# Another order of the first loads in a two-layer trunk: one modulation piece ahead of x, small tables moved to SyncE's queue

## The chip, the cores and the metric

The kernel runs on 1 core of one Trainium2 chip. The metric is the device time of one execution in microseconds (us): the median of several runs. One more execution is taken with the hardware profiler; the trace and every row below come from that one. The engines are TensorE (PE in the rows, with its weight loads as PEld), VectorE (DVE), ScalarE (ACT), GpSimd (POOL) and SyncE (SP, which only issues transfers here).

## The reference, cut to what matters

What is computed is a trunk of two layers over 128 context tokens and 512 latent tokens (640 columns), model width 1024. The part that the change touches is the beginning of layer 0:

```python
def rms_norm(x, g):
    xf = x.astype(jnp.float32)
    y = xf * lax.rsqrt(jnp.mean(xf * xf, axis=-1, keepdims=True) + EPS)
    return (y * g.astype(jnp.float32)).astype(x.dtype)

def modulation(cvec, w, b):
    m = jax.nn.silu(cvec) @ w + b
    return jnp.split(m[:, None, :], N_MOD, axis=-1)
...
        hp = rms_norm(xp, norm1) * (1 + sc1_p) + sh1_p
        hs = rms_norm(xs, norm1) * (1 + sc1_s) + sh1_s
        if layer % 2 == 0:
            mp, new_k, new_v = attn_mixer_context(hp, l0_w_in, ...)
            ms = attn_mixer_latent(hs, cache_l0_k, cache_l0_v, l0_w_in, ...)
```

`attn_project` multiplies the normalised x with `l0_w_in` and splits the columns into q, k, v of grouped-query attention (mixer A, with a rotary on the latent tokens' q and k) and q, k, v of a neighbourhood attention (mixer B). Then come the output projection, a squared-ReLU MLP, and layer 1 (a gated delta rule and another MLP).

## The kernel before

**Two phases.** `net_kernel` (L1551) builds two phases. The first (L1559 to L1564) holds the setup, the first norm and modulation, and all of layer 0's attention (`attn_layer`, L586). It is built with `schedule_with_timeline_sim=True`: a scheduler sets, when the kernel is built, the order of instructions on each engine from its own estimate of times, so the order isn't the order of the code. The second phase is in the order of the code. Between them is a barrier: TensorE's first matmul of phase two waits for the branch at L78 that ends phase one.

**The first norm.** `first_norm` (L310) works feature-major: x arrives as 8 tiles of 128 x 640 (320 KB each; tile k holds features 128k to 128k+127, columns 0 to 511 are latent and 512 to 639 context). Its loads go to SyncE's queue, one behind the other: x (L320), then the modulation weights for shift and scale in 4 pieces of 2 MB (L324; "m0" to "m3" below, in a pool of 3 buffers, so m3 waits until m0 is read). Between m1 and m2 the call `use(None, None)` puts the first 256 columns of `w_in0`, the k and v columns of mixer A (`proj_w`, L608 to L612; 1 MB, "w0" below, then w1, w2, ... for the q columns). Each w is split into a high part (ACT, L228) and a low part (DVE, L229), in two halves, t_79/t_80 and t_81/t_82 for w0.

**The arithmetic of the head.** The squares of x are summed (`sumsq`, ACT L295 and L298, DVE L299, into `acc`), a matmul with ones sums over partitions (L306, bank kq), and ACT makes the reciprocal root `rs` (L307, L308). A piece s of the modulation (64 small matmuls, L340, bank md; a copy, L343; a transposition, L345; gains on DVE, L348 and L350) gives shift and scale for features k = 2s and 2s+1. For k below 4, DVE multiplies x by gain and rs (L357), ACT adds the shift and rounds to the high part (L358), DVE makes the low part (L359). For k from 4 on DVE multiplies by rs first (L363), gain and shift follow (L366 on DVE, L369 on ACT), and `split_act` (L235, L236) makes the two parts. The parts of k are t_59+2k (high) and t_60+2k (low).

**The projection.** Every k goes straight into the k/v projection: for each of 5 token blocks three matmuls (L618 high by high, L619 high x by low w, L620 low x by high w), into three banks that stay open over all k: pj_122 (blocks 0 and 1), pj_123 (2 and 3), pj_124 (4). Beside them the first q columns are projected block by block, into pj_699 (block 0), md_738 (block 1), md_777 (block 2), and pj_816 (block 3). The banks named pj are four buffers in rotation, so pj_816 is written where pj_122 was: it waits until `ev_kv` has read blocks 0 and 1 out (split of v on ACT L605, the norm of k: ACT L681, L684, L685, DVE L683, L686; then rotary, L705 and L708, and a transposition on PE, L735).

**Tables and cache.** The rotary table `rope` (256 KB, L662), and the context's k (`cka`, L713, 128 KB) and v (`cv`, L715, 64 KB) are loaded by ACT's queue at the kernel's start. DVE multiplies `rope` with the k and q gains into two tables (L668, L673); the tables are first needed by the rotary behind the k norm.

**Further on** in phase one: mixer A, then mixer B from about 262 us, in whose course further modulation weights (`t<-in_mod_w_dram`, matmuls of L170) are loaded and used. Scores are L981 to L985, their transpositions L789, outputs L842, L924, L1007 and L1017.

Of the kernel before, what the change touches and what calls it, by code (L numbers as in the profile page):

```python
# [11 lines left out]
F32 = mybir.dt.float32  # L12
# [6 lines left out]
P = 128  # L19
D = 1024  # L20
NK = D // P
TS = 512
TP = 128
T = TS + TP
# [25 lines left out]
class Net:  # L50
# [259 lines left out]
    def first_norm(self, use):  # L310

        nc = self.nc
        w = self.i["mod_w0"]
        with ExitStack() as c:
            mp = c.enter_context(self.tc.tile_pool(name="m0", bufs=3))
            self.open_norm(c)
            xt, ws = [], []
            for k in range(NK):
                t = self.xp.tile([P, T], F32, tag="x", name="x")
                nc.sync.dma_start(out=t, in_=self.i["xT"][k * P:(k + 1) * P, :])  # L320
                xt.append(t)
            for s in range(4):
                wt = mp.tile([P, NK, 512], F32, tag="w", name="w")
                nc.sync.dma_start(out=wt, in_=w[:, s * 512:(s + 1) * 512].rearrange("(k p) c -> p k c", p=P))  # L324
                ws.append(wt)
                if s == 1:
                    use(None, None)
            for k in range(NK):
                self.sumsq(k, xt[k], 0, T)
            rs = self.np.tile([P, T], F32, tag="rs", name="rs", bufs=1)  # L330
            for hf in range(2):
                self.rsqrt(rs, hf, "kq")
            g = self.gain[0, 0]
            by_block = lambda z: z.rearrange("p (i k) -> p k i", i=2)
            for s in range(4):
                two = slice(2 * s, 2 * s + 2)
                ps = self.bank("md")
                for k in range(NK):
                    for q in range(4):
                        nc.tensor.matmul(ps[32 * q:32 * q + 32, 0:P], lhsT=self.cs[:, k, :], rhs=ws[s][:, k, q * P:(q + 1) * P],  # L340
                                         start=(k == 0), stop=(k == NK - 1))
                m = self.sm.tile([P, P], F32, tag="modm", name="modm", bufs=1)
                nc.scalar.copy(m, ps[:, 0:P])  # L343
                pt = self.bank("md")
                nc.tensor.transpose(out=pt[:, 0:P], in_=m, identity=self.ident)  # L345
                ptv = pt[:, 0:P].rearrange("p (k i x) -> p k i x", k=2, i=2)
                for v in range(2):
                    nc.vector.tensor_tensor(out=by_block(self.modT[0][:, 0:16, v])[:, two], in0=ptv[:, :, :, v],  # L348
                                            in1=by_block(self.vec("modb0")[:, 0:16])[:, two], op=ALU.add)
                    nc.vector.scalar_tensor_tensor(out=g[:, two, v], in0=self.modT[0][:, 8 + 2 * s:10 + 2 * s, v], scalar=1.0,  # L350
                                                   in1=self.vec("n1_0")[:, two], op0=ALU.add, op1=ALU.mult)
                for k in (2 * s, 2 * s + 1):
                    if k < 4:
                        x, (hi, lo) = xt[k], self.act[2 * k:2 * k + 2]
                        for v, o in ((0, slice(0, TS)), (1, slice(TS, T))):
                            sh = self.mod_vec(0, 0, k, v)
                            nc.vector.scalar_tensor_tensor(out=x[:, o], in0=x[:, o], scalar=g[:, k, v:v + 1], in1=rs[:, o], op0=ALU.mult, op1=ALU.mult)  # L357
                            nc.scalar.activation(hi[:, o], x[:, o], AF.Identity, bias=sh)  # L358
                            nc.vector.scalar_tensor_tensor(out=lo[:, o], in0=x[:, o], scalar=sh, in1=hi[:, o].bitcast(F32),  # L359
                                                           op0=ALU.add, op1=ALU.subtract)  # L360
                        use(k, (hi, lo))
                        continue
                    nc.vector.tensor_tensor(out=xt[k], in0=xt[k], in1=rs, op=ALU.mult)  # L363
                    for v, o in ((0, slice(0, TS)), (1, slice(TS, T))):
                        if k % 2:
                            nc.vector.tensor_scalar(out=xt[k][:, o], in0=xt[k][:, o], scalar1=g[:, k, v:v + 1],  # L366
                                                    scalar2=self.mod_vec(0, 0, k, v), op0=ALU.mult, op1=ALU.add)
                        else:
                            nc.scalar.activation(xt[k][:, o], xt[k][:, o], AF.Identity, scale=g[:, k, v:v + 1], bias=self.mod_vec(0, 0, k, v))  # L369
                    use(k, self.split_act(k, xt[k]))  # L370
# [215 lines left out]
def attn_layer(n):  # L586
# [44 lines left out]
    with ExitStack() as outer:  # L631
# [27 lines left out]
        with c:  # L659
            tp = c.enter_context(tc.tile_pool(name="qt", bufs=2))  # L660
            rope = tp.tile([P, 4, 128], F32, name="rope", bufs=1)
            nc.scalar.dma_start(out=rope, in_=I["rope"])  # L662

            tabs = {}
            for nm in ("gqa_r", "gkan_r"):
# [44 lines left out]

            nc.scalar.dma_start(out=vall[:, 5, :], in_=I["ctxv"][:, 128:640])
            ck = tp.tile([P, KVA, 128], F32, name="cka", bufs=1)
            nc.scalar.dma_start(out=ck, in_=I["ctxk"][:, 0:KVA])  # L713
            cv = tp.tile([P, 128], F32, name="cv", bufs=1)
            nc.scalar.dma_start(out=cv, in_=I["ctxv"][:, 0:128])  # L715
            split_v(va[5], cv)
            kd = [tp.tile([P, KVA, 2, HD], F32, name=f"ka{blk}", bufs=1) for blk in range(NB)]

# [1026 lines left out]
```

## Time and profile before

| what | value |
|---|---|
| median of 3 runs | 1807.68 us |
| lowest and highest run | 1805.96 and 1809.21 us |
| the profiled execution's own time | 1806.72 us |
| its span, first to last instruction | 1805.0 us |
| mean granted TensorE clock over the span | 0.992 of full speed |
| TensorE busy | 1726.7 us, 96 % of the span |
| DVE, ACT, GpSimd busy | 70 %, 51 %, 12 % |
| bytes moved | 187.22 MB, mean 104 GB/s |
| first matmul of phase two | at 344.57 us |

How to read it: TensorE is busy nearly all the time, so the end is set by where TensorE idles or runs at the lower of its two clocks (1.2 instead of 2.4 GHz, shown as 0.50 and 1.00 of full speed). In the page's rows a slice is 45 us long; only the first, with a busy share of five tenths, is far from full, and the DMA engines are full there and nearly idle afterwards. The change lies in that slice.

### The profile page before, as it was taken

The page shows a single profiled execution, that of the slowest core. Times are in us where ns is not written, and L with a number is a line of the kernel's source. Part 1 is how long each engine was busy: PE and PEld are TensorE (multiplying, and loading weights), DVE is VectorE, ACT ScalarE, POOL GpSimd, SP SyncE. Part 2 cuts the span into 40 slices and gives each one's busy share as a digit, 9 for nine tenths or more (in the row PEclk, how much of TensorE's full clock was granted, in tenths as well). Part 3 has the DMA queues.
Part 4 walks back from the last instruction along what each step waited for, and adds up shares of the span by engine and source line. Part 5 has one row for each costly group of instructions (what it writes and reads, how often), then busy time and mean ns, then how long its engine had stood idle before and what let it go on. Part 6 is the DMA issues. An engine that isn't in the chain of part 4 may idle for free. (4 is left out here: it accounts for less than half of the span.)

```text
span 1805.0 us, 34898 instructions
## 1 busy us (share of the span) xinstructions
PE 1726.7 (96%) x14120; PEld 1621.2 (90%) x14120; DVE 1266.6 (70%) x2554; ACT 921.0 (51%) x2037; POOL 215.1 (12%) x218
## 2 busy tenths in 40 slices
PE   5999998899999999999989999999999999999999
PEld 4898886699999999999888878878999999999999
DVE  6766557469988678787697877776449957465562
ACT  4555565345345171554756656656636427164360
POOL 0233314100000000000232222222110000000000
PEclk9999998999999999999999999999999999999999
DMA  9101059314433435254122222232232423222231
GB/s 351 57 27 50 26 157 284 132 52 164 164 117 125 135 101 200 73 178 162 48 48 70 50 48 69 51 82 73 66 129 94 140 63 101 72 71 94 68 104 52
DMA packets 174994, 187.22 MB, mean 104 GB/s; under 512 B 48457, under 2 KB 152137, under 8 KB 174833
## 3 DMA queue, kind: packets, MB, share of 16 engines
q1 hardware_dynamic: 170272, 175.05, 30.9%
q0 software_dynamic: 1408, 5.41, 0.9%
q10 hardware_dynamic: 3152, 4.52, 0.8%
q8 instruction: 111, 1.82, 0.4%
q14 instruction: 51, 0.41, 0.1%
HBM read 170.97 MB, written 11.37 MB: 101 GB/s over the span
## 5 line engine op out<-in xcount | busy, mean ns | idle before, releaser
L228 ACT CAST t<-t 128x1024 fp32r<-128x1024 f32 x169 | 176.5, 1048 | 243.0 <-PE p L246 135.7
L229 DVE TENSOR_TENSOR t<-t 128x1024 fp32r<-128x1024 f32 x169 | 207.3, 1230 | 56.8 <-ACT t L228 55.9
L245 PE MATMUL dn<-t 128*128 128x320 f32 x648 | 207.7, 320 | 3.7 <-PEq L78 3.1
L246 PE MATMUL dn<-t 128*128 128x320 f32 x648 | 208.2, 321 | 0.0
L247 PE MATMUL dn<-t 128*128 128x320 f32 x648 | 207.4, 320 | 0.0
L246 PE MATMUL p<-hl,t 128*128 128x320 f32 x448 | 138.5, 309 | 0.0
L245 PEld LDWEIGHTS dn<-t 128*128 128x128 f32 x648 | 122.5, 189 | 7.9 <-issue 5.8
L246 PE MATMUL dn<-hl,t 128*128 128x320 f32 x416 | 129.0, 310 | 0.0
L192 DVE SCALAR_TENSOR_TENSOR ma<-t,ma 128x1024 f32<-128x1024 f32 x98 | 122.8, 1279 | 6.0 <-DMA t<-in_mod_w_dram 5.8
L246 PEld LDWEIGHTS dn<-t 128*128 128x128 f32 x648 | 122.6, 189 | 4.0 <-issue 2.5
L247 PEld LDWEIGHTS dn<-t 128*128 128x128 f32 x648 | 122.6, 189 | 3.4 <-issue 2.5
L413 DVE SCALAR_TENSOR_TENSOR x<-p,t,x 128x192 f32<-128x192 f32 (+2 forms) x154 | 53.1, 385 | 101.0 <-PE p L247 101.0
L245 PE MATMUL p<-hh,t 128*128 128x320 f32 x392 | 121.3, 310 | 0.0
L247 PE MATMUL p<-hh,t 128*128 128x320 f32 x392 | 121.2, 309 | 0.0
L245 PE MATMUL dn<-hh,t 128*128 128x320 f32 x376 | 116.8, 311 | 0.0
L247 PE MATMUL dn<-hh,t 128*128 128x320 f32 x376 | 116.2, 309 | 0.0
L228 ACT CAST wxh<-t 128x1024 fp32r<-128x1024 f32 x49 | 51.3, 1047 | 85.9 <-PE p L246 40.6
L413 DVE SCALAR_TENSOR_TENSOR x<-dn,t,x 128x320 f32<-128x320 f32 (+1 forms) x86 | 44.9, 525 | 62.4 <-PE dn L247 51.8
L246 PEld LDWEIGHTS p<-hl,t 128*128 128x128 f32 x448 | 84.1, 188 | 0.0
L246 PEld LDWEIGHTS dn<-hl,t 128*128 128x128 f32 x416 | 78.1, 188 | 1.0 <-issue 0.8
L783 POOL TENSOR_TENSOR p<-p,smx 128x640 f32<-128x640 f32 (+1 forms) x48 | 63.8, 1338 | 114.9 <-DVE smx L782 99.3
L245 PEld LDWEIGHTS p<-hh,t 128*128 128x128 f32 x392 | 73.6, 188 | 0.8 <-issue 0.4
(599 smaller groups left out, 5195.7 us busy)
## 6 DMA issues: line engine op xcount, KB each, us to landing
t<-in_mlp_w_dram SPq DMA_DIRECT2D x64, 1024.0 KB
t<-in_mod_w_dram SPq DMA_DIRECT2D x40, 1024.0 KB, 6.4
t<-in_w_qkv_dram SPq DMA_DIRECT2D x12, 1024.0 KB
t<-in_w_in_dram SPq DMA_DIRECT2D x9, 1024.0 KB, 5.4
w<-in_mod_w_dram SPq DMA_DIRECT2D x4, 2048.0 KB, 16.3
t<-in_w_out_dram SPq DMA_DIRECT2D x8, 1024.0 KB, 5.7
bias<-in_biasx_dram SPq DMA_DIRECT2D x8, 512.0 KB, 6.7
t<-in_w_z_dram SPq DMA_DIRECT2D x4, 1024.0 KB
```

Of the source, the lines that this page charges most:

```text
L192: nc.vector.scalar_tensor_tensor(out=acc[v], in0=wt[:, k], scalar=c, in1=acc[v], op0=ALU.mult, op1=ALU.add)
L228: nc.scalar.copy(hi, raw)
L229: nc.vector.tensor_tensor(out=lo, in0=raw, in1=hi.bitcast(F32), op=ALU.subtract)
L245: self.nc.tensor.matmul(ps, lhsT=hi[:, k, :], rhs=xh[:, ts_], start=(k == 0), stop=False)
L246: self.nc.tensor.matmul(ps, lhsT=hi[:, k, :], rhs=xl[:, ts_], start=False, stop=False)
L247: self.nc.tensor.matmul(ps, lhsT=lo[:, k, :], rhs=xh[:, ts_], start=False, stop=(k == NK - 1))
L413: nc.vector.scalar_tensor_tensor(out=xout[:, a:b], in0=ps[:, a - o:b - o], scalar=self.mod_vec(layer, idx, k, v), in1=xin[:, a:b], op0=ALU ...
L783: nc.gpsimd.tensor_tensor(out=pv, in0=pv, in1=sm.unsqueeze(2).broadcast_to([P, nb, w]), op=ALU.mult)
```

## The change

`first_norm` writes its loads in another order, and three small loads go from ACT's queue to SyncE's. The piece of modulation m0 is loaded first, then x, then w0, then m1, m2, m3. The code of one piece of modulation is put into a function (same instructions), and m0's is called ahead of the sums of squares. The transfers' sizes and the arithmetic are the same. Since phase one's order is chosen when the kernel is built, every engine's order in phase one changes.

```diff
             xt, ws = [], []
-            for k in range(NK):
-                t = self.xp.tile([P, T], F32, tag="x", name="x")
-                nc.sync.dma_start(out=t, in_=self.i["xT"][k * P:(k + 1) * P, :])
-                xt.append(t)
-            for s in range(4):
+            g = self.gain[0, 0]
+            by_block = lambda z: z.rearrange("p (i k) -> p k i", i=2)
+
+            def load(s):
                 wt = mp.tile([P, NK, 512], F32, tag="w", name="w")
                 nc.sync.dma_start(out=wt, in_=w[:, s * 512:(s + 1) * 512].rearrange("(k p) c -> p k c", p=P))
                 ws.append(wt)
-                if s == 1:
-                    use(None, None)
-            for k in range(NK):
-                self.sumsq(k, xt[k], 0, T)
-            rs = self.np.tile([P, T], F32, tag="rs", name="rs", bufs=1)
-            for hf in range(2):
-                self.rsqrt(rs, hf, "kq")
-            g = self.gain[0, 0]
-            by_block = lambda z: z.rearrange("p (i k) -> p k i", i=2)
-            for s in range(4):
+
+            def modulation(s):
+
                 two = slice(2 * s, 2 * s + 2)
                 ps = self.bank("md")
...
+
+            load(0)
+            for k in range(NK):
+                t = self.xp.tile([P, T], F32, tag="x", name="x")
+                nc.sync.dma_start(out=t, in_=self.i["xT"][k * P:(k + 1) * P, :])
+                xt.append(t)
+            use(None, None)
+            for s in range(1, 4):
+                load(s)
+            modulation(0)
+            for k in range(NK):
+                self.sumsq(k, xt[k], 0, T)
+            rs = self.np.tile([P, T], F32, tag="rs", name="rs", bufs=1)
+            for hf in range(2):
+                self.rsqrt(rs, hf, "kq")
+            for s in range(4):
+                if s:
+                    modulation(s)
                 for k in (2 * s, 2 * s + 1):
...
-            nc.scalar.dma_start(out=rope, in_=I["rope"])
+            nc.sync.dma_start(out=rope, in_=I["rope"])
...
-            nc.scalar.dma_start(out=ck, in_=I["ctxk"][:, 0:KVA])
+            nc.sync.dma_start(out=ck, in_=I["ctxk"][:, 0:KVA])
             cv = tp.tile([P, 128], F32, name="cv", bufs=1)
-            nc.scalar.dma_start(out=cv, in_=I["ctxv"][:, 0:128])
+            nc.sync.dma_start(out=cv, in_=I["ctxv"][:, 0:128])
```

In the changed kernel line numbers are shifted: L320 is L348, L324 is L323, L340 to L350 are L332 to L342, L357 to L369 are L367 to L379, and everything from `attn_layer` on is 10 lines later.

**SyncE's queue**, from its first transfer on (x, w of modulation, t of `w_in0` = w0, w1, ...). Before:

```order
L101 DMA craw<-in_cT_dram 128x16
L102 DMA t<-in_vecs_dram 128x333
L320 DMA x<-in_xT_dram 128x640 x8
L324 DMA w<-in_mod_w_dram 128x8x512 x2
L611 DMA t<-in_w_in_dram 128x8x256
L324 DMA w<-in_mod_w_dram 128x8x512
L611 DMA t<-in_w_in_dram 128x8x256
L324 DMA w<-in_mod_w_dram 128x8x512
L611 DMA t<-in_w_in_dram 128x8x256 x3
```

And now:

```order
L101 DMA craw<-in_cT_dram 128x16
L102 DMA t<-in_vecs_dram 128x333
L323 DMA w<-in_mod_w_dram 128x8x512
L348 DMA x<-in_xT_dram 128x640 x8
L621 DMA t<-in_w_in_dram 128x8x256
L323 DMA w<-in_mod_w_dram 128x8x512 x2
L672 DMA rope<-in_rope_dram 128x512
L723 DMA cka<-in_ctxk_dram 128x256
L725 DMA cv<-in_ctxv_dram 128x128
L621 DMA t<-in_w_in_dram 128x8x256
L323 DMA w<-in_mod_w_dram 128x8x512
L621 DMA t<-in_w_in_dram 128x8x256 x3
```

m0 has moved ahead of x, w0 ahead of m1, and rope, cka and cv stand behind m2 and ahead of w1; m3 has the same bytes ahead of it as before.

**DVE in the head**: the rotary tables (`tbgqa_r`, `tbgkan_r`) against the sums of squares (`acc`) and the normalised x. Before, from the setup's last instruction on:

```order
L107 TENSOR_TENSOR t<-craw,ce 128x8x2
L668 TENSOR_TENSOR tbgqa_r<-rope,t 128x4x64
L673 TENSOR_TENSOR tbgqa_r<-rope,t 128x4x16 x4
L668 TENSOR_TENSOR tbgkan_r<-rope,t 128x4x64
L673 TENSOR_TENSOR tbgkan_r<-rope,t 128x4x16 x4
L299 TENSOR_TENSOR acc<-acc,sq 128x640 x7
L363 TENSOR_TENSOR x<-x,rs 128x640 x4
L348 TENSOR_TENSOR t<-md,t 128x2x2 x2
```

And now, from the first normalised k on (`acc` and w0's low parts stand ahead of this):

```order
L373 TENSOR_TENSOR x<-x,rs 128x640 x4
L369 SCALAR_TENSOR_TENSOR t<-x,t 128x512
L369 SCALAR_TENSOR_TENSOR t<-x,t 128x128
L369 SCALAR_TENSOR_TENSOR t<-x,t 128x512
L369 SCALAR_TENSOR_TENSOR t<-x,t 128x128
L678 TENSOR_TENSOR tbgqa_r<-rope,t 128x4x64
L683 TENSOR_TENSOR tbgqa_r<-rope,t 128x4x16 x4
L678 TENSOR_TENSOR tbgkan_r<-rope,t 128x4x64
L683 TENSOR_TENSOR tbgkan_r<-rope,t 128x4x16 x4
L340 TENSOR_TENSOR t<-md,t 128x2x2 x2
L342 SCALAR_TENSOR_TENSOR t<-t 128x2 x2
```

The rotary tables moved from the very start to a place between the low parts of k = 0, 1 and the gains (L340) of k = 2, 3.

**PE at the k/v projection's last features**, k = 6 (t_71, t_72) and k = 7 (t_73, t_74). Before, where k = 6 begins:

```order
L620 MATMUL md_738<-t_79,t_70 128x256
L618 MATMUL md_777<-t_83,t_59 128x256
L619 MATMUL md_777<-t_84,t_59 128x256
L620 MATMUL md_777<-t_83,t_60 128x256
L618 MATMUL md_777<-t_83,t_61 128x256
L618 MATMUL pj_122<-t_81,t_71 128x256
L619 MATMUL pj_122<-t_82,t_71 128x256
```

And now:

```order
L629 MATMUL md_777<-t_84,t_65 128x256
L630 MATMUL md_777<-t_83,t_66 128x256
L628 MATMUL md_777<-t_79,t_67 128x256
L629 MATMUL md_777<-t_80,t_67 128x256
L630 MATMUL md_777<-t_79,t_68 128x256
L628 MATMUL md_777<-t_79,t_69 128x256
L629 MATMUL md_777<-t_80,t_69 128x256
L630 MATMUL md_777<-t_79,t_70 128x256
L628 MATMUL pj_122<-t_81,t_71 128x256
L629 MATMUL pj_122<-t_82,t_71 128x256
```

Fourteen more of the matmuls of q's block 2 (md_777) now stand ahead of k = 6 of the k/v projection. From the last matmul into pj_122 to the first transposition of k (L735, now L745), behind which pj_816 begins, there were 38 matmuls; now there are 21.

## Rows read from the trace of the kernel before

**Rows 1.** The page: busy us, share of the span, instructions, of TensorE.

```profile
PE 1726.7 (96%) x14120; PEld 1621.2 (90%) x14120; DVE 1266.6 (70%) x2554; ACT 921.0 (51%) x2037; POOL 215.1 (12%) x218
```

**Rows 2.** TensorE in time: start, us, instruction, idle before it and who ended it.

```profile
14.66 2.50 PE L306 MATMUL kq<-acc,t 128*128 128x320 f32 x4 [14.66 <-DVE acc L299]
17.83 3.20 PE L340 MATMUL md<-w,t 128*32 128x128 f32 x64 [0.67 <-DMA w<-in_mod_w_dram]
...
23.36 3.22 PE L340 MATMUL md<-w,t 128*32 128x128 f32 x64 [1.54 <-DMA w<-in_mod_w_dram]
27.34 0.62 PE L618 MATMUL pj<-t 128*128 128x256 f32 x3 [0.75 <-ACT t L228]
...
28.60 0.39 PE L619 MATMUL pj<-t 128*128 128x256 f32 x1
...
40.18 0.27 PE L345 MATMUL md<-t,modm 128*128 128x128 f32 x1
41.54 1.95 PE L340 MATMUL md<-w,t 128*32 128x128 f32 x64 [1.09 <-DMA w<-in_mod_w_dram]
...
58.78 0.33 PE L735 MATMUL kq<-t,ka 128*128 128x128 f32 x1 [0.60 <-DVE ka L708]
60.01 0.36 PE L618 MATMUL pj<-t 128*128 128x256 f32 x1 [0.90 <-DVE kn L686]
```

**Rows 3.** DMA issues to 100 us: transfer, queue, count, KB each, median us to landing.

```profile
w<-in_mod_w_dram SPq DMA_DIRECT2D x4, 2048.0 KB, 16.3
...
rope<-in_rope_dram ACTq DMA_DIRECT2D x1, 256.0 KB, 2.8
```

**Rows 4.** ACT in time, columns as in rows 2.

```profile
6.13 0.74 ACT L295 ACTIVATE acc<-x 128x640 f32<-128x640 f32 x1 [2.81 <-DMA x<-in_xT_dram]
...
17.75 0.47 ACT L308 ACTIVATE rs<-rs 128x320 f32<-128x320 f32 x1
...
23.04 1.97 ACT L358 ACTIVATE t<-x,t 128x512 fp32r<-128x512 f32 x4 [1.66 <-DVE x L357]
26.24 1.99 ACT L228 CAST t<-t 128x1024 fp32r<-128x1024 f32 x2 [1.24 <-DMA t<-in_w_in_dram]
...
53.66 0.27 ACT L605 CAST va<-pj 128x128 fp32r<-128x128 f32 x1 [5.81 <-PE pj L620]
```

**Rows 5.** DVE in time, columns as in rows 2.

```profile
4.43 0.42 DVE L668 TENSOR_TENSOR tbgqa_r<-rope,t 128x256 f32<-128x256 f32 x1 [0.40 <-DMA t<-in_vecs_dram]
...
5.65 0.62 DVE L673 TENSOR_TENSOR tbgkan_r<-rope,t 128x64 f32<-128x64 f32 x4
...
18.26 3.03 DVE L363 TENSOR_TENSOR x<-x,rs 128x640 f32<-128x640 f32 x4 [3.65 <-ACT rs L308]
```

**Rows 6.** Stretches: length, busy us of PE, PEld, DVE, ACT, POOL, PEclk, DMA share, GB/s.

```profile
20.40:23.85 3.45, 1.42 (x42) 1.02 (x37) 2.88 (x10) 1.08 (x3) 0.00 (x0) 1.00 1.06 368
23.85:27.27 3.42, 2.73 (x55) 2.28 (x44) 2.19 (x6) 2.19 (x5) 0.00 (x0) 0.50 1.07 371
...
57.90:61.40 3.50, 2.00 (x16) 1.63 (x15) 2.85 (x13) 1.86 (x9) 1.68 (x6) 1.00 0.00 0
61.40:81.90 20.50, 20.50 (x172) 20.26 (x171) 20.06 (x52) 12.64 (x42) 9.38 (x17) 1.00 0.21 59
81.90:85.30 3.40, 1.55 (x12) 1.07 (x11) 3.02 (x4) 2.94 (x7) 1.57 (x2) 1.00 0.23 42
85.30:92.10 6.80, 5.77 (x27) 5.80 (x28) 3.79 (x7) 3.95 (x8) 0.00 (x0) 0.50 0.39 134
```

**Rows 7.** TensorE's waits, 262 to 342 us: for whom, us in total, times, longest.

```profile
PE dn L170 <- DMA t<-in_mod_w_dram: 5.6, 3, 3.7
PE dn L245 <- PEq L78: 3.1, 1, 3.1
PE t L789 <- DVE t L998: 2.3, 1, 2.3
```

**Rows 8.** A stretch in mixer B, columns as in rows 6.

```profile
283.30:293.50 10.20, 7.97 (x45) 6.25 (x46) 5.88 (x10) 3.89 (x10) 3.98 (x3) 0.50 1.04 309
```

## The prediction

> **What bounds the kernel now.** I read the page first: TensorE is busy for 96 % of the span [rows 1], so the time moves only where TensorE idles or runs at half clock. Phase two waits for phase one at a barrier and isn't touched; what counts is when phase one's last work ends. So I read TensorE in time from the start: what ends each idle stretch? [rows 2] Until 14.66 us it has nothing (it waits for the sum of squares). Then it waits 0.67 and 1.54 us for modulation pieces m0 and m1, 0.75 us for w0's high part, and 1.09 us for m3 at 41.54. Between these it has work. The loads are the limit up to there: the DMA share is 1.06 and 1.07 in the two stretches shown, at some 370 GB/s [rows 6]. Behind 41.54 the next wait is at 58.78 (0.60 us) and 60.01 (0.90 us), both for the k norm and rotary of the first blocks, not for a load [rows 2]. The reader should see that the end of the head is not where the loads' order is decided: m3 is the last load that TensorE waits for.
>
> **The loads.** All loads share one stream, so I shift arrivals by bytes. m0 and m1 (2.10 MB each) were met 23.36 - 17.83 = 5.53 us apart [rows 2], so 1 MB takes 2.64 us; x takes 6.9 us, a w 2.8, rope, cka and cv together (0.46 MB) 1.2. Before, m0 was met at 17.83 with x, m0 and the small loads done. Now x is the last of the same bytes, less the three small loads: 17.83 - 1.2 = 16.6 for x's last tile, and 9.7 for m0. Forward from there: w0 19.4, m1 24.9, m2 30.5, rope 31.2. Backward from m3, which has the same bytes ahead of it and so stays at 41.54: w1 36.0, rope to cv 33.2, m2 32.0. The two ways differ by 1.5 us; I take the middle: x 17.2, w0 20, m1 25.5, m2 31.2, rope 32, m3 41.5.
>
> **Sum of squares and w0.** m0's matmuls now run ahead of x's end, at no cost. The sum of squares, whose end released TensorE at 14.66 [rows 2], ends at about 18.7 (x comes 5 us later, but DVE has less to catch up with). From there the row chain is 18.26 - 14.66 = 3.6 us to `rs` [rows 5]. Before that end ACT now has the casts of w0 (1.99 us, [rows 4]), which wait for w0; so `rs` comes at about 23.4 instead of 18.22. The first k/v matmul then starts near 25 (0.75 us of L357 and 0.7 of L358 behind it) against 27.34. That is an advantage of some 2.4 us, but low parts follow only at about 29, against 28.60: DVE puts four normalisations (3.03 us, [rows 5]) ahead of them. So k = 0, 1 end near 32, as before, and nothing is gained or lost here.
>
> **The rotary tables.** Before, they cost nothing: 1.84 us of DVE from 4.43 to 6.27, ahead of the first square [rows 5]. Now they stand in DVE's row ahead of the gains of k = 2, 3 and wait for rope, which is queued behind all of x, m0, w0, m1 and m2. DVE is held from about 31.9, when it could make the gains, to 32 + 1.84 = 33.9; behind it wait the gains (0.46), L357 (0.75) and L358 (0.7), so k = 2's first matmul starts at about 35.9. TensorE has m2's modulation (1.95 at full clock, [rows 2]) to do meanwhile, until about 34.15. It idles 1.75 us. Bounds: 0 if rope lands 2 us earlier; 2.4 if it lands 0.7 later, at the backward bound. Then some 45 matmuls at 20.50 / 172 = 0.119 us [rows 6] lead to the state which before was reached by 40.18 (+ 0.27): I get 41.6. Before, TensorE then waited for m3 until 41.54. So this stall eats the slack in front of m3 and shifts the rest by only 0.1 us: **+0.1**.
>
> **The clock behind that stall.** After stretches with 1.42 and 1.55 us of work in 3.4 us the granted clock was 0.50 for 3.4 and 6.8 us; after one with 2.00 in 3.5 it stayed at 1.00 [rows 6]. With 1.75 us idle, and some gaps around m2's matmuls, the stretch here has about 1.6, nearer to the first two. A fall of 3.4 us of dense work costs half of that, 1.7; bounds 0 and half of the 5.77 busy us in the longer fall, 2.9. I take **+1.7**.
>
> **The order of k/v against q.** Between 41.5 and 58 TensorE has the same work in both kernels, but q's block 2 now stands ahead of k = 6, 7 of the k/v projection. The first bank, pj_122, is finished with only 21 matmuls left to do instead of 38. From the read-out of that bank (ACT L605 at 53.66, [rows 4]) to the start of pj_816, which reuses it (60.01, [rows 2]), the chain through ACT and DVE takes 6.35 us; its instructions are the same. Before, TensorE idled 0.60 + 0.90 of these. Now 17 matmuls fewer cover it: 17 x 0.119 = **+2.0**. Bounds: 0 if DVE and ACT, with other work around, run the chain 2 us faster; 3.9 if the k = 6 parts also come late by the stall's 1.9.
>
> **The clock behind that gap.** TensorE now idles 1.5 + 2.0 = 3.5 us there within 5. The stretch that before had 2.00 busy and kept its clock [rows 6] would have under 1: it falls below those after which the clock was halved. What follows was solid work (20.50 of 20.50, [rows 6]), so again 1.7, bounds 0 and 3.4 (6.8 us of solid work at half): **+1.7**.
>
> **62 to 262 us.** Up to mixer A the order differs by five transpositions which stand earlier; I put that at **+0.4** (five at 0.14 by the chain's shape, less what the wait loses), bounds -1 and +2. Mixer A itself has the same order. The 0.50 stretch at 85.30 is there in both.
>
> **Mixer B** (262 to 341 us) is ordered anew: transpositions and outputs of the first heads stand between scores, and the modulation groups of L170 are shifted. TensorE waited there 5.6 us for modulation weights and 2.3 us for the last DVE step [rows 7], and ran 10.20 us at half clock behind the longest of these waits, with 7.97 us busy [rows 8]. No row tells how the new order stands to them. From below: all 5.6 us and half of 7.97 come back, -9.6. From above: the order makes one more wait of the size of the longest (3.7) and a tail of 1.3: +5. I take 0, since the loads' stream and the same sums of work remain.
>
> **A rule weighed.** Before, rope was issued on ACT's queue at 0.8 us and landed 2.8 us later, while x's and m0's transfers were being queued on SyncE's; a transfer on SyncE's queue that stood behind others took 16.3 us [rows 3]. The Trainium skill ("DMA: Bandwidth & Descriptors", section "Queues, rings and completion order") says that each DMA engine takes turns between the queue rows that have work, and works each row's ring in order. By that, a small load on ACT's queue passes the 10 MB on SyncE's, and moving it there is what makes it late: left where it was, the sum would be smaller by the clock's 1.7 and the 0.1. The trace agrees with its 2.8 against 16.3.
>
> **The sum.** 0.1 + 1.7 + 2.0 + 1.7 + 0.4 + 0 = +5.9 us. Against the profiled execution's own 1806.72 this gives 1812.6; that execution lies 0.96 below the median of the runs, 1807.68, from which it would be 1813.6. I say **1813**. The runs lie within 3.25 us, so about 0.2 % (3.6 us) is what a measurement of this kernel can tell from no change: faster is below 1804.1, slower above 1811.3.
>
> **Rivals.**
> - *The clock holds* in both places: 0.1 + 2.0 + 0.4 = 2.5, 1809.2 to 1810.2, no difference to be told. For it: the stretch with 2.00 busy kept its clock. Against: the gap ahead of pj_816 leaves less. Chance 0.22.
> - *Faster: mixer B's new order covers the waits for modulation weights.* If L170's groups stand later against their transfers, up to 5.6 us of waits and 4.0 us of half clock vanish. It decides once more than 5.9 + 3.6 = 9.5 of these 9.6 come back, or with no clock fall in the head (+2.5) once 6.1 do, which means the wait of 3.7 and the slow stretch behind it. All of it with the clock holding: 1807 + 2.5 - 9.6 = 1800; half of that stretch left: 1802. Chance 0.17.
> - *Rope isn't late*, that is, the change doesn't put it where its place in the queue says: the transfers of one queue overlap, it is small, and lands before 30. Then the first fall goes too: 2.0 + 1.7 + 0.4 = 4.1, 1811 to 1812. Chance 0.08.
> - *Mixer B gets worse* by its +5: 1818. Chance 0.08.
> - The forecast itself, 1813, give or take 2: 0.45.
>
> **How the numbers follow.** The faster case gives 0.16. Same: 0.22 from the clock rival, and 0.06 from the lower edge of the forecast and of the rope case: 0.28. Slower: 0.56. The range leaves out half of the faster case and the far end of the worst: 1802 to 1819.
>
> **What would show it.** In the changed kernel: TensorE's first matmul of m0 near 10 us and first k/v matmul near 25; DVE's L678 waiting for a DMA until about 32 and TensorE idle for some 1.7 us before k = 2; no wait for m3 at 41.5; pj_816 (L628 after L745) starting at 62 to 65 instead of 60.01, with DVE as its releaser and an idle time of 3 us or more; granted clock 0.50 behind it. Phase two's first matmul at about 350 instead of 344.57. I am wrong if that matmul comes before 344, if the k norm's chain runs much faster, or if mixer B's waits for modulation weights change by more than 3 us.

## The result, and the profile after

The changed kernel takes 1819.14 us (median of 5 runs, 1816.24 to 1821.43), against 1807.68 before (by now five runs as well): the medians lie 11.5 us apart. The ratio, estimated from all the runs, is 1.0056, with a 95 % interval of 1.0041 to 1.0071. So it is slower by about 10 us. The profiled execution has a span of 1814.5 us, 9.5 more than before's 1805.0; it is the fastest of the five.

TensorE in time, as in [rows 2]. In the changed kernel L332 is a modulation piece (before L340), L628 to L630 the projections, L745 the transpositions:

```profile
9.90 3.64 PE L332 MATMUL md<-w,t 128*32 128x128 f32 x64 [9.90 <-DMA w<-in_mod_w_dram]
...
18.66 2.50 PE L306 MATMUL kq<-acc,t 128*128 128x320 f32 x4 [3.18 <-DVE acc L299]
24.56 0.58 PE L628 MATMUL pj<-t 128*128 128x256 f32 x1 [3.39 <-ACT t L368]
24.94 0.41 PE L629 MATMUL pj<-t 128*128 128x256 f32 x1
...
26.14 3.48 PE L332 MATMUL md<-w,t 128*32 128x128 f32 x62
...
29.77 0.28 PE L628 MATMUL pj<-t 128*128 128x256 f32 x1
...
33.24 1.96 PE L332 MATMUL md<-w,t 128*32 128x128 f32 x64
...
36.08 0.38 PE L628 MATMUL pj<-t 128*128 128x256 f32 x1 [0.89 <-ACT t L368]
...
61.51 0.33 PE L745 MATMUL kq<-t,ka 128*128 128x128 f32 x1 [2.64 <-DVE ka L718]
62.74 0.35 PE L628 MATMUL pj<-t 128*128 128x256 f32 x1 [0.90 <-DVE kn L696]
...
90.38 0.33 PE L745 MATMUL kq<-t,ya 128*128 128x128 f32 x1 [2.91 <-DVE ya L718]
92.83 1.51 PE L745 MATMUL kq<-t,ya 128*128 128x128 f32 x6 [2.12 <-DVE ya L705]
...
352.90 0.39 PE L245 MATMUL dn<-t 128*128 128x320 f32 x1 [3.25 <-PEq L78]
```

No row waits for m1, m2 or m3 any more. The first k/v matmul comes at 24.56 instead of 27.34, pj_816 (62.74) 2.73 us later than before, and phase two's first matmul (352.90) 8.33 later. The waits at 58.78 and 60.01 of [rows 2], 0.60 and 0.90 us, are 2.64 and 0.90 now.

VectorE's first step on rope, the rope transfer (as in [rows 3]), and ACT's first read-out of a k/v bank (before at 53.66, [rows 4]):

```profile
32.37 0.42 DVE L678 TENSOR_TENSOR tbgqa_r<-rope,t 128x256 f32<-128x256 f32 x1 [2.64 <-DMA rope<-in_rope_dram]
rope<-in_rope_dram SPq DMA_DIRECT2D x1, 256.0 KB, 15.9
56.40 0.27 ACT L615 CAST va<-pj 128x128 fp32r<-128x128 f32 x1 [4.47 <-PE pj L630]
```

Three stretches (columns as in [rows 6]), and TensorE's waits in mixer B (as in [rows 7]):

```profile
24.50:29.30 4.80, 4.74 (x65) 4.28 (x68) 4.80 (x9) 1.22 (x4) 0.00 (x0) 1.00 1.05 388
57.90:62.70 4.80, 1.30 (x10) 0.91 (x8) 3.49 (x11) 2.62 (x10) 0.73 (x3) 1.00 0.00 0
62.70:66.90 4.20, 4.16 (x22) 4.19 (x23) 4.16 (x17) 2.96 (x15) 1.95 (x6) 0.59 0.02 4
PE dn L170 <- DMA t<-in_mod_w_dram: 5.3, 2, 2.8
PE t L799 <- DVE t L1008: 4.0, 1, 4.0
```

The clock falls behind the gap ahead of pj_816 (mean 0.59 of full speed over 62.70 to 66.90). Up to 29.3 us TensorE works at half its later pace (64 matmuls of modulation take 3.64 us at 9.90 and 1.96 at 33.24), although the profile gives its granted clock as 1.00 there. In mixer B the modulation weights are still waited for, 5.3 against 5.6 us, and the last wait for VectorE is 4.0 instead of 2.3.

To compare kernels by stage, four moments on TensorE are enough, each the start of one row: pj_816's first matmul, mixer A's first projection (the first dn), mixer B's first score, phase two's first matmul.

| kernel | pj_816 | mixer A | mixer B | phase two | end of span |
|---|---|---|---|---|---|
| before | 60.01 | 87.50 | 262.03 | 344.57 | 1805.0 |
| changed | 62.74 | 94.82 | 268.42 | 352.90 | 1814.5 |
| e1 rope on ACT | 64.52 | 96.59 | 271.89 | 359.20 | 1821.3 |
| e2 k/v first | 61.14 | 93.24 | 268.57 | 354.42 | 1818.1 |
| e3 old tail | 62.56 | 91.96 | 266.50 | 351.16 | 1817.0 |
| e4 both | 61.31 | 89.62 | 264.32 | 348.21 | 1816.3 |
| e5 loads only | 65.18 | 92.68 | 264.32 | 346.36 | 1810.4 |
| e6 rope only | 65.41 | 92.48 | 266.51 | 349.63 | 1809.6 |
| e7 changed, tail moved | 62.56 | 92.09 | 267.25 | 355.21 | 1816.9 |
| e8 before, tail moved | 59.13 | 85.04 | 257.92 | 341.65 | 1804.8 |
| e9 m3 first | 57.87 | 83.43 | 256.33 | 341.22 | 1805.4 |
| e10 new mixer B | 60.56 | 87.64 | 260.06 | 347.39 | 1812.8 |

By differences along the first two lines, the 9.5 us are: +2.7 up to pj_816, +4.6 from there to mixer A, -0.9 in mixer A, +1.9 in mixer B, +1.2 in phase two. The last is not the change's: phase two takes 1460.0 to 1468.1 us in these twelve executions, though its instructions are the same, with 3.4 us at half clock in the shortest and 17 in the longest. So the end of one span says little about 2 or 3 us. The moments up to phase two say more, but they vary too: with the same order in the head, pj_816 came at 60.01, 59.13 and 60.56 (before, e8, e10), and mixer A, whose order is the same in all, takes 171.6 to 175.3 us. Whether a kernel is faster is said by the ratios of the timed runs.

### The profile page after: what moved, and what is told of

Read it like the earlier page. It is cut to its first block, busy times and chain, and to the rows that moved or that the text cites. A ratio compares the mean times of both kernels' runs of the same rounds, so it can differ in the third digit from the quotient of the medians.

```text
span 1814.5 us, 34889 instructions
## 1 busy us (share of the span) xinstructions
PE 1732.8 (95%) x14120; PEld 1625.4 (90%) x14120; DVE 1266.5 (70%) x2554; ACT 919.5 (51%) x2037; POOL 215.8 (12%) x218
## 4 chain that ended last, share of the span: by engine, by line
PE 64%; DVE 10%; ACT 3%; issue 2%; DMA 1%; POOL 0%; SPq 0%; DVEq 0%; ACTq 0%; POOLq 0%
PE dn L245 7%; PE dn L246 7%; PE dn L247 7%; PE dn L484 7%; PE p L247 6%; PE p L245 6%; PE p L246 6%; PE p L484 5%; PE s L484 5%; DVE ma L192 2%; DMA t<-in_mod_w_dram 1%; PE p L1450 1%; DVE t L229 1%; PE p L1459 1%; DVE at L1310 1%
```

## The experiments

In phase one a change of a line moves the whole order, since the scheduler chooses again. To change one thing at a time, these kernels carry a table with the order of every engine's instructions in phase one, taken from before or from the changed kernel; it orders their issue only. Their line numbers are 20 higher than in the kernel they start from.

**e1: the changed kernel's order, rope on ACT's queue.**

```diff
-            nc.sync.dma_start(out=rope, in_=I["rope"])
+            nc.scalar.dma_start(out=rope, in_=I["rope"])
...
-            nc.sync.dma_start(out=ck, in_=I["ctxk"][:, 0:KVA])
+            nc.scalar.dma_start(out=ck, in_=I["ctxk"][:, 0:KVA])
...
-            nc.sync.dma_start(out=cv, in_=I["ctxv"][:, 0:128])
+            nc.scalar.dma_start(out=cv, in_=I["ctxv"][:, 0:128])
```

> The changed kernel with its own order of instructions on every engine, fixed by a table, but with rope, cka and cv on ACT's queue at the start, as before. Only the arrival of the three small loads differs. Theory (orders): the late rope costs at most the 0.89 us that TensorE idles ahead of k = 2 (36.08 us); the k/v bank is still finished late, so pj_816 starts at 61.8 to 62.7 us with some 3.5 us of idle time ahead of it, and phase two's first matmul comes at 352 to 353. Rival (rope): the stall of VectorE by rope is what delays the head; then pj_816 starts near 60 and phase two at 348 or earlier.

Measured: 1822.09 us, ratio to before 1.0074 (1.0056 to 1.0092). The wait ahead of k = 2 is gone (0.11 us are left of 0.89), yet pj_816 comes later, at 64.52. TensorE's rows, m0, the sum of squares and the first k/v matmul:

```profile
11.89 3.64 PE L352 MATMUL md<-w,t 128*32 128x128 f32 x64 [11.89 <-DMA w<-in_mod_w_dram]
20.66 2.50 PE L326 MATMUL kq<-acc,t 128*128 128x320 f32 x4 [3.33 <-DVE acc L319]
26.58 0.58 PE L648 MATMUL pj<-t 128*128 128x256 f32 x1 [3.41 <-ACT t L388]
```

All three are 2.0 us later than in the changed kernel (9.90, 18.66, 24.56). The loads on ACT's queue land early (rope in 2.8 us), but m0 lands 10.0 us after its issue instead of 8.0 (10.4 in e5, which has the three loads there too), and the first matmuls wait for m0 and x. The granted clock is then 0.50 from 18.9 to 32.6 us. Late rope can cost at most the 0.89 us that TensorE idled ahead of k = 2, and neither theory had the price of loading it early.

**e2: k/v ahead of q's block 2.** TensorE's order only:

```diff
+L628 MATMUL pj_122<-t_81,t_71 128x256
+L629 MATMUL pj_122<-t_82,t_71 128x256
...
 L629 MATMUL md_777<-t_84,t_61 128x256
 L630 MATMUL md_777<-t_83,t_62 128x256
...
-L628 MATMUL pj_122<-t_81,t_71 128x256
-L629 MATMUL pj_122<-t_82,t_71 128x256
```

> The changed kernel with one difference: on TensorE, the 65 matmuls from q's block 2 (md_777) up to the first transposition of k stand in the order of before, so k = 6, 7 of the k/v projection come ahead of most of block 2. Theory (orders): pj_816 starts 1.5 to 2.5 us earlier, at 60.2 to 61.2 us, the clock does not fall behind it, mixer A starts 3 to 4.4 us earlier than 94.82, and phase two at 348.5 to 350. Rival (data late): the parts of k = 6, 7 are not there that early, TensorE waits for them instead, and pj_816 stays at 62 or later, phase two at 352 to 353.

Measured: 1820.16 us, ratio 1.0069 (1.0047 to 1.0091). The gap closes and the clock holds:

```profile
59.91 0.33 PE L765 MATMUL kq<-t,ka 128*128 128x128 f32 x1 [0.61 <-DVE ka L738]
61.14 0.36 PE L648 MATMUL pj<-t 128*128 128x256 f32 x1 [0.90 <-DVE kn L716]
```

```profile
61.10:88.80 27.70, 23.42 (x190) 22.68 (x190) 24.41 (x60) 14.65 (x48) 12.39 (x22) 1.00 0.14 44
```

pj_816 is 1.6 us earlier, as expected. But mixer A is 1.6 earlier too, not 3 to 4.4: from pj_816 to mixer A it takes 32.10 us with the clock at 1.00, and 32.08 in the changed kernel with the fall. TensorE is busy for only 23.42 of 27.70 us there and doesn't set the pace, so the half clock cost nothing in this order. Behind that the gain is lost in stages whose order is the changed kernel's: mixer B starts at 268.57 (268.42) and phase two at 354.42 (352.90), beyond what either theory said. The timed runs show no gain.

**e3: the old order behind the k/v read-out.** From there to the end of phase one every engine and SyncE's queue have the order of before. One place of VectorE's:

```diff
 L710 TENSOR_TENSOR t1_1028<-z_1020,tbgqa_r_555
+L693 TENSOR_REDUCE ss_1062<-sq_1060
 L718 TENSOR_TENSOR ya_909<-t1_1028,t2_1029
-L693 TENSOR_REDUCE ss_1062<-sq_1060
 L696 TENSOR_TENSOR z_1059<-pj_1034,ss_1062
```

> The changed kernel with its own order up to the read-out of the k/v banks, and from there to the end of phase one the order of before on TensorE, VectorE, ACT and GpSimd, and on SyncE behind the last projection load. Theory (orders): pj_816 stays at 62.7 us and the clock falls behind it, but the stretch up to mixer A gets back its 2.9 us (mixer A starts near 92 instead of 94.82), and mixer B its 1.0: phase two at 348.5 to 349.5. Rival (data late): the tail waits as long as now, since its waits come from the shift of the head: phase two at 352 to 353.

Measured: 1813.82 us, ratio 1.0028 (1.0015 to 1.0040). The two waits ahead of mixer A are as long as in the kernel before, in place of 2.91 and 2.12 us. Before's rows:

```profile
84.15 0.66 PE L735 MATMUL kq<-t,ya 128*128 128x128 f32 x4 [1.36 <-ACT qaT L755]
86.33 1.51 PE L735 MATMUL kq<-t,ya 128*128 128x128 f32 x6 [1.52 <-DVE ya L695]
```

Mixer A starts at 91.96, as expected; phase two at 351.16, not 348.5 to 349.5. The timed runs show half of the loss gone.

**e4: e2 and e3 together.** From q's block 2 on the order of before, with the loads and the head's order of the change:

```diff
+L628 MATMUL pj_122<-t_81,t_71 128x256
...
 L630 MATMUL md_777<-t_83,t_62 128x256
...
+L693 TENSOR_REDUCE ss_1062<-sq_1060
 L718 TENSOR_TENSOR ya_909<-t1_1028,t2_1029
-L693 TENSOR_REDUCE ss_1062<-sq_1060
```

> The changed kernel's loads and its own order up to q's block 2, and from there the order of before on every engine (the two edits before this one together). Theory (orders): pj_816 at 60.2 to 61.2 us, mixer A at 87.5 to 88.7 and phase two at 344.6 to 346, so the time is that of before within 0.1 per cent, with the loads still in their new order and rope still late. Rival (loads): if the new order of the loads or the late rope costs time of its own, phase two stays at 348 or later.

Measured: 1811.62 us, ratio 1.0021 (1.0007 to 1.0035). pj_816 at 61.31, mixer A at 89.62, phase two at 348.21: about 2 us later than before at mixer A, so the theory's 344.6 to 346 is missed and the rival's 348 is met. Of the changed kernel's 0.56 %, the orders from q's block 2 on account for 0.35; the loads, with the head's own order, for a rest of 0.21. With the old order behind the read-out, the clock's fall does cost something: from pj_816 to mixer A it takes 29.40 us in e3, where the clock falls at 62.4, and 28.31 here, where it holds.

**e5: the loads' order alone.** Before, with SyncE's queue changed and nothing else:

```diff
+L324 DMA w<-in_mod_w_dram 128x8x512
 L320 DMA x<-in_xT_dram 128x640 x8
-L324 DMA w<-in_mod_w_dram 128x8x512 x2
 L611 DMA t<-in_w_in_dram 128x8x256
-L324 DMA w<-in_mod_w_dram 128x8x512
+L324 DMA w<-in_mod_w_dram 128x8x512 x2
 L611 DMA t<-in_w_in_dram 128x8x256
```

> The kernel before with one difference: SyncE's queue holds m0, x, w0, m1, m2, w1, m3 in the changed kernel's order; rope, cka and cv stay on ACT's queue, and every compute engine keeps the order of before. Theory (orders): the new order of the loads costs next to nothing by itself, since m3 has the same bytes ahead of it: m0 is met near 12 us and the sum of squares ends near 20.7 (as in the run with rope on ACT's queue), the first k/v matmul comes at 28 to 30 instead of 27.34, m3's modulation at 41.5 to 43, pj_816 at 60 to 61.5, phase two at 344.5 to 346.5. Rival (loads): the later sum of squares shifts everything behind it; pj_816 at 62.5 or later, phase two at 348 or later.

Measured: 1813.41 us, ratio 1.0018 (1.0005 to 1.0030). Up to pj_816 the rival was right:

```profile
31.74 0.61 PE L638 MATMUL pj<-t 128*128 128x256 f32 x3 [2.42 <-ACT t L248]
...
35.94 0.41 PE L639 MATMUL pj<-t 128*128 128x256 f32 x1
...
36.45 0.28 PE L639 MATMUL pj<-t 128*128 128x256 f32 x1
...
48.58 0.39 PE L638 MATMUL pj<-t 128*128 128x256 f32 x1 [1.04 <-ACT t L255]
...
65.18 0.35 PE L638 MATMUL pj<-t 128*128 128x256 f32 x1 [0.90 <-DVE kn L706]
```

The first k/v matmul is 4.40 us later than before and pj_816 5.17 later. Before, TensorE waits behind that matmul 1.09 us for m3 [rows 2] and 0.55 for m2:

```profile
33.12 0.64 PE L340 MATMUL md<-w,t 128*32 128x128 f32 x14 [0.55 <-DMA w<-in_mod_w_dram]
```

Both waits are gone here, so 1.6 us of the delay are absorbed. Two losses come on top: the clock is at 0.50 from 32.8 to 36.2 us, on the k/v matmuls (before from 23.9 to 27.3, ahead of them), which costs about 1.3, an estimate from the time between the first k/v matmul and m3's first one (13.84 against 14.20 - 1.64); and the parts of k = 6 are waited for (1.04). Phase two, at 346.36, is only 1.8 later than before and inside the theory's range, since mixer A took 171.6 us instead of 174.5; by the timed runs the loads' order costs 0.18 %.

**e6: rope alone.** Before, with rope, cka and cv on SyncE's queue behind m2, and the tables where the changed kernel has them:

```diff
-L668 TENSOR_TENSOR tbgqa_r<-rope,t 128x4x64
...
 L229 TENSOR_TENSOR t<-t 128x1024 x2
+L668 TENSOR_TENSOR tbgqa_r<-rope,t 128x4x64
...
 L348 TENSOR_TENSOR t<-md,t 128x2x2 x2
```

> The kernel before with one difference: rope, cka and cv stand on SyncE's queue behind m2, and VectorE makes the rotary tables where the changed kernel does, between w0's low parts and the gains of k = 2, 3. Theory (orders): VectorE waits for rope until about 32 us, k = 2 starts near 36, and TensorE's wait for m3 (1.09 us) is gone in exchange, so pj_816 comes at 60 to 61.5 and phase two at 344.5 to 346.5. Rival (rope): the stall is passed on in full; pj_816 at 62.5 or later and phase two at 348 or later.

Measured: 1812.41 us, ratio 1.0029 (1.0014 to 1.0044). TensorE at k = 2 and pj_816:

```profile
36.42 0.39 PE L638 MATMUL pj<-t 128*128 128x256 f32 x1 [3.39 <-ACT t L378]
65.41 0.36 PE L638 MATMUL pj<-t 128*128 128x256 f32 x1 [0.90 <-DVE kn L706]
```

Here the rival was right: k = 2 waits 3.39 us, and pj_816 is 5.40 late. Not all of that is the wait: the clock is at 0.50 from 27.6 to 31.0 and again from 37.9 to 41.3 us, which by the same estimate costs 2.8 together, and the wait of 1.04 for k = 6 is there too; the waits for m2 and m3 (1.6) are gone. At pj_816 each half of the change costs more alone, in the old order, than both together in the scheduler's new one (2.73): in the head the new order helps.

**e7: the changed kernel with four moves ahead of mixer A.** VectorE's part:

```diff
+L693 TENSOR_REDUCE ss_1062<-sq_1060
 L718 TENSOR_TENSOR ya_909<-t1_1028,t2_1029
-L693 TENSOR_REDUCE ss_1062<-sq_1060
...
-L229 TENSOR_TENSOR t_82<-t_78,t_81
 L718 TENSOR_TENSOR ya_910<-t1_1067,t2_1068
...
-L229 TENSOR_TENSOR t_84<-t_77,t_83
...
 L705 TENSOR_TENSOR ya_911<-z_1098,t_52
+L229 TENSOR_TENSOR t_82<-t_78,t_81
+L229 TENSOR_TENSOR t_84<-t_77,t_83
```

> The changed kernel with four moves in the last q blocks before mixer A: on VectorE the sum of squares of block 3 stands ahead of the rotary addition of block 2, and the two subtractions of the next weights' low parts (1.2 us each) stand behind the last q block; on ACT the last norm's two steps stand ahead of a copy of q, and one cast of weights behind it. TensorE's order is the changed kernel's. Theory: the 2.9 us lost ahead of mixer A are the vector engines' order: TensorE's two transposition groups start at about 88.5 and 90.3 us instead of 90.38 and 92.83, GpSimd's rotary of block 3 takes 1.1 us instead of 2.02 since VectorE's subtraction is no longer beside it, and mixer A starts at 92 to 93 instead of 94.82. Rival: TensorE's own order, with transpositions ahead of the last block, costs them; then mixer A stays at 94.3 or later.

Measured: 1818.76 us, ratio 1.0044 (1.0029 to 1.0060). TensorE's two groups, and GpSimd's rotary of block 3:

```profile
88.20 0.33 PE L765 MATMUL kq<-t,ya 128*128 128x128 f32 x1 [0.91 <-DVE ya L738]
90.10 1.51 PE L765 MATMUL kq<-t,ya 128*128 128x128 f32 x6 [1.58 <-DVE ya L725]
86.64 1.05 POOL L735 TENSOR_TENSOR t<-z,tbgqa_r 128x128 f32<-128x128 f32 x2 [0.94 <-DVE z L716]
```

In the changed kernel this last row was

```profile
87.84 2.02 POOL L715 TENSOR_TENSOR t<-z,tbgqa_r 128x128 f32<-128x128 f32 x2 [1.96 <-DVE z L696]
```

Mixer A starts at 92.09 instead of 94.82, so 2.7 us come back with TensorE's order as it was. But they aren't all a cost of the change, since GpSimd's last rotary lies beside a subtraction in the kernel before, too, and is as slow:

```profile
81.44 2.03 POOL L705 TENSOR_TENSOR t<-z,tbgqa_r 128x128 f32<-128x128 f32 x2 [1.23 <-DVE z L686]
```

What the change brought is the place of the sum of squares. Block 3's norm on VectorE, in the changed kernel and in e7:

```profile
87.28 0.42 DVE L696 TENSOR_TENSOR z<-pj,ss 128x256 f32<-128x256 f32 x1 [0.60 <-ACT ss L695]
86.08 0.42 DVE L716 TENSOR_TENSOR z<-pj,ss 128x256 f32<-128x256 f32 x1
```

That is 1.2 us earlier, 0.2 of it from the head. Phase two then came at 355.21, later than the changed kernel's: mixer B, in the same order, took 88.0 us. The ratio's interval overlaps the changed kernel's, so the timed runs don't show the gain.

**e8: the same place in the kernel before.**

```diff
-L229 TENSOR_TENSOR t_82<-t_78,t_81
 L708 TENSOR_TENSOR ya_910<-t1_1067,t2_1068
...
-L229 TENSOR_TENSOR t_84<-t_77,t_83
...
 L695 TENSOR_TENSOR ya_911<-z_1098,t_52
+L229 TENSOR_TENSOR t_82<-t_78,t_81
+L229 TENSOR_TENSOR t_84<-t_77,t_83
```

> The kernel before with three moves at the same place: VectorE's two subtractions of the next weights' low parts stand behind the last q block's norm, and one of ACT's casts of weights behind the last norm's two steps. Theory: TensorE's two waits of 1.36 and 1.52 us ahead of mixer A shrink to 0.7 to 0.9 each, GpSimd's rotary of block 3 takes 1.1 us instead of 2.03, and mixer A starts at 86.0 to 86.7 instead of 87.50; if the clock then also holds (it fell at 85.3 us before), a further 2 to 3 us come back, phase two at 340.5 to 343.5. Rival: the subtractions are needed by mixer A's first projections, and what is gained is waited for there; phase two at 344 or later.

Measured: 1808.00 us, ratio 0.9995 (0.9983 to 1.0007), no difference that the runs can tell. The two waits shrink, and the clock holds there:

```profile
82.50 0.66 PE L755 MATMUL kq<-t,ya 128*128 128x128 f32 x4 [0.58 <-ACT qaT L775]
84.09 1.19 PE L755 MATMUL kq<-t,ya 128*128 128x128 f32 x6 [0.94 <-ACT t L248]
```

From pj_816 to mixer A it takes 25.91 instead of 27.49 us (27.07 to 27.50 in before, e5, e6 and e10). So these moves gain over 1 us in the old order as well.

**e9: a version from these findings.** Before, with e8's moves, and:

```diff
 L324 DMA w<-in_mod_w_dram 128x8x512
-L611 DMA t<-in_w_in_dram 128x8x256
 L324 DMA w<-in_mod_w_dram 128x8x512
+L611 DMA t<-in_w_in_dram 128x8x256
...
 L340 MATMUL md_439<-w_158,t_75 32x128 x32
 L618 MATMUL pj_122<-t_81,t_67 128x256
...
 L620 MATMUL pj_124<-t_81,t_74 128x256
 L618 MATMUL pj_699<-t_83,t_59 128x256
```

> A version of the kernel before, built on what the runs so far showed: SyncE's queue has m3 ahead of w1 (one swap); TensorE's order has all matmuls of the k/v projection ahead of q's blocks 0 to 2, m2's modulation in one piece and m3's ahead of k = 4; the splits of w1 on ACT and VectorE stand behind the parts of k = 6, 7; and the three moves of the run before it ahead of mixer A. Everything from mixer A on is as before. Theory (the head's shifts pass through once the wait for m3 is used up, and the k/v bank's read-out must be covered): m3 is met near 38.7 us instead of 41.54, the k/v banks are finished near 48.5 instead of 53.7, TensorE has no wait ahead of pj_816, which starts at 57 to 58 instead of 60.01, mixer A at 82.8 to 84.5 instead of 87.50, phase two at 340 to 342 instead of 344.57: a ratio of 0.997 to 0.999. Rival (mixer B absorbs it): its loads of modulation weights are met later instead, phase two at 344 or later and no difference in the time.

Measured: 1804.77 us, ratio 0.9972 (0.9962 to 0.9983): faster than before, and so than the changed kernel. ACT's read-out of the first bank and pj_816, which nothing holds up:

```profile
48.31 0.27 ACT L625 CAST va<-pj 128x128 fp32r<-128x128 f32 x1 [1.21 <-PE pj L640]
57.87 0.36 PE L638 MATMUL pj<-t 128*128 128x256 f32 x1
```

**e10: mixer B's new order in the kernel before.** One place, TensorE's outputs and scores (in the kernel before's line numbers):

```diff
-L789 MATMUL t<-t,p 128x128 x4
-L1017 MATMUL o<-pt,vall 128*64 x2
 L826 MATMUL t<-t,qs 128x128 x2
...
+L981 MATMUL sc<-kk,qs 128x256
+L985 MATMUL sc<-ckb,qs 128x128
...
 L153 MATMUL dn<-t,modm 128x128 x2
```

> The kernel before with one difference: from mixer A's first projection on, every engine and SyncE's queue has the changed kernel's order, which differs from before in mixer B alone. Loads, head and q blocks are as before. Theory: mixer B's new order costs time of its own; from its first scores to phase two the four kernels with the new order took 84.5, 87.3, 85.9 and 88.0 us, the six with the old one 82.0 to 84.7. So mixer A starts at 87 to 88 as before, phase two comes at 346.5 to 349 instead of 344.57, and the ratio is 1.001 to 1.002. Rival: the difference came from where the half-clock stretches happened to fall; then phase two at 343.5 to 345.5 and the ratio within 0.001 of 1.

Measured: 1813.06 us, ratio 1.0017 (1.0006 to 1.0028). Mixer A starts at 87.64, phase two comes at 347.39. TensorE's waits from 260 to 349 us:

```profile
PE dn L190 <- DMA t<-in_mod_w_dram: 6.7, 2, 3.9
PE t L809 <- DVE t L1018: 4.0, 1, 4.0
...
PE o L944 <- DVE kbT L941: 1.9, 1, 1.9
```

The order costs some 3 us by itself (1 to 5 by the interval). In the kernel before these three waits are 5.6, 2.3 [rows 7] and 0.7 us. The last wait for VectorE is 4.0 us as in the changed kernel: the last scores stand right ahead of it there, at 328.76 us, while before 5 us of other work followed them, so less is left to cover their softmax. The rival doesn't explain it: in mixer B the clock is at half for 10.2 us in both kernels. In the twelve executions mixer B takes 82.0 to 84.9 us with the old order (seven) and 84.5 to 88.0 with the new (five).

## Why the prediction was right or wrong

**The time.** I said 1813, within 1802 to 1819; it was 1819.14, at the upper end of that range. The spans lie 9.5 us apart, and I had 5.9. Up to pj_816 it was 2.7 where I had 3.8; the clock's fall behind it, 1.7 by me, cost nothing; and 6.5 us came up to mixer A and in mixer B, where I had 0.4 and 0. So the direction was right, and the mechanism of the head in part, but that the whole still fell near the range's end is luck: terms too large and terms left out made up for each other.

**Right: the direction, and the head's course.** Loads shifted by bytes gave m0 at 9.7 (9.90), the sum of squares at 18.7 (18.66), the first k/v matmul near 25 (24.56), rope at 32 (32.37), k = 2 at 35.9 (36.08), no wait for m3, and 3.5 us idle ahead of pj_816 (2.64 + 0.90). The k/v-against-q term, 2.0 us, is borne out at pj_816 by e2, which got 1.6 back there with that order alone; the timed runs don't show it.

**Wrong: "the end of the head is not where the loads' order is decided".** Since m3 has the same bytes ahead of it, I priced the loads at nothing. In the old order e5 shows 5.2 us at pj_816 for them and e6 5.4 for rope, in both with a part that is the clock's. Behind the first k/v matmul TensorE waits for loads only 1.6 us in all (I had overlooked the 0.55 for m2), so m3 was hardly a limit. The scheduler's new order absorbed most of it; e4 leaves 1.3, of which some can be the spread between executions (59.13 to 60.56 with the order of before).

**Wrong: the clock behind rope's stall, +1.7.** No half-clock stretch came there. The idle time was 0.89, not 1.75 us, since TensorE was itself later: its first k/v matmuls took 0.41 us each against 0.28 from 29.77 on, and m1's 62 took 3.48 us, all at the half pace that lasted until 29.3. Before, the half pace lay on m1's modulation, ahead of the k/v start. That this is the 1.3 us of e4 is argued, not tested. In sum I had 3.8 up to pj_816; it was 2.7. That k = 2 came on time is luck in part: a shorter wait stood behind a slower start.

**Wrong: the price of the clock's fall behind the gap, +1.7.** The fall came (0.59 over that stretch), but cost nothing in the changed kernel: by e2, what follows takes as long with the clock at full. With the old order behind the read-out the fall goes with 1.1 us (e3 against e4).

**Wrong: "62 to 262 us", +0.4 with bounds -1 and +2.** From pj_816 to mixer A it was +4.6. I compared TensorE's rows alone and counted five transpositions. With the old order of all engines 2.7 of it come back (e3 against the changed kernel), and 3.8 where the clock holds (e4 against e2). One part is located: the sum of squares of q's block 3 stands behind the rotary addition of block 2, which waits for GpSimd; moving it brings block 3's norm 1.0 us forward (e7). The rest of e7's 2.7 comes with moves that gain over 1 us in the old order, too (e8). Whether the remaining loss is TensorE's order or the other engines' isn't shown. Mixer A itself was -0.9, less than the 3.7 us by which it varies.

**Wrong: mixer B, taken at 0.** It was +1.9 in the profiled execution; against e3, which has the old order there, it isn't seen (84.5 against 84.7 us). e10 prices its order at 0.17 %, 3.1 us of 1809 (interval 1.1 to 5.1), within the bound of +5 that I had set. That this is why the medians lie 11.5 us apart and the two spans 9.5 is possible, but not shown.

**The rivals.** That the clock holds was right behind rope's stall and wrong behind the gap ahead of pj_816, where its fall cost nothing. The rope that isn't late: it was late. The faster case, mixer B's new order covering its loads, fails: 5.3 against 5.6 us of these waits, and a longer wait at the end. Mixer B getting worse (1818) came nearest to the time, but mixer B gave only 1.9 of the 9.5 us.

**The rule weighed.** On ACT's queue rope does pass the others: 2.8 us to landing in e1, against 15.9. What the Trainium skill ("DMA: Bandwidth & Descriptors", "Queues, rings and completion order") says of queues taking turns agrees with that. The conclusion that rope there would make the sum smaller is refuted: m0, the sum of squares and the first k/v matmul came 2.0 us later, and pj_816 1.8. That fits turns taken from m0 and x; but by bytes the three loads are worth 1.2 us (the prediction's estimate), and where the other 0.8 comes from is open.

**What stays open.** Mixer B took 84.5, 87.3, 85.9, 88.0 and 87.3 us with the same order in five kernels; which of its waits moves with the time at which it starts wasn't tried.

## What to carry to other kernels

When a scheduler orders a stage, compare every engine's row, not only the busiest one's: here the order behind the read-out cost 2.7 to 3.8 us up to mixer A, while TensorE's row alone had suggested 0.4. To find which part of a change costs what, fix the order by a table and move one thing at a time; and look whether a move gains as much in the kernel before, since then it isn't the change's cost. A load that is last doesn't make earlier ones free: ask how much idle time lies between their users and its own, since only that much delay is absorbed (here 1.6 us). And work that needs a long read-out, as the k/v banks do, goes ahead of work that can cover it: with m3's load moved up, k/v first and e8's moves, e9 gained 0.28 %. Which of the three gained it wasn't taken apart; e8's moves alone gave no difference that the runs can tell.

## What the runs showed of the hardware

GpSimd's two rotary multiplications of block 3 take 2.02 us together in the changed kernel (87.84) and 2.03 before (81.44), where VectorE's subtraction of 1024 columns ran beside them; with the subtraction moved away, 1.05 (e7 and e8). The Trainium skill ("SBUF — State Buffer", "Who interferes with whom") says that a VectorE instruction with two inputs in SBUF contends with a GpSimd instruction that reads SBUF; the trace agrees.

What a fall of the granted clock costs depends on whether TensorE sets the pace: with the new order the stretch from pj_816 to mixer A takes 32.10 us without a fall behind pj_816 (e2), 32.08 with 3.4 us at 0.50 and 32.07 with 6.8 (e1). With the old order, where TensorE idles less, it takes 28.31 without (e4) and 29.40 with 3.4 (e3). And phase two, the same instructions in all twelve executions, varied by 8 us.
